# Later weight sums, another unit order and shifted forms in a one-core transformer layer

## The chip, the cores and the metric

The kernel runs on one core of one Trainium2 chip. The metric is the device time of one execution in microseconds; the number given for a kernel is the median of its runs. A profiled execution is a separate run, recorded instruction by instruction; its own time stands beside the span that the profile covers.

## The reference

One layer for 272 tokens (16 learned meta tokens ahead of 256 real ones) of 2048 features: a SwiGLU half-step, a mixer with two kinds of attention, and a second SwiGLU half-step. The meta tokens are dropped at the end. All is float32.

```
h = concatenate([meta, x])
h = h + 0.5 * swiglu(rmsnorm(h, ffn1_norm), w_gate1, w_up1, w_down1)     # D_FF = 5632
h = h + hybrid_mixer(rmsnorm(h, mix_norm), w_in, ..., w_out)             # fox + stick-breaking heads
h = h + 0.5 * swiglu(rmsnorm(h, ffn2_norm), w_gate2, w_up2, w_down2)
swiglu(x) = (silu(x @ w_gate) * (x @ w_up)) @ w_down
```

## The kernel before, in words

**Units.** All weight matrices are read once, in units of 128 x 1024 float32 values (512 KB). `load` (line 1118) brings a unit from memory into a `raw` tile by a DMA on SP's queue. `split_unit` (line 1131) makes two halves of it in a reduced float format: `wh`, a rounded copy by ScalarE (lines 189 and 1136), and `wl = raw - wh` by VectorE (lines 190 and 1142). `products` (line 1174) multiplies: for every float32 product TensorE runs three matmuls, high by high, high by low and low by high. `wh` and `wl` have three buffers each, so a copy into one waits for the unit three places earlier. The loop at the end calls `ahead(u)` and `products(u)` for every unit `u`; `ahead` (line 1232) loads 6 units ahead (9 in the second half-step) and splits 2 units ahead. `raw` has 5 buffers, and 3 more in the second half-step.

**Order.** The list `units` gives the order in which the program is traced. The framework's scheduler then orders each engine's instructions by that priority and by its own estimate of when operands are ready, so an instruction can come before others that were traced earlier. Each engine's queue runs in order, SP's with its DMAs too. `tc.issue_after(i)` keeps what follows behind instruction `i` on `i`'s queue. The first units are traced under a manual schedule for ScalarE and VectorE.

**First half-step.** 264 units of 24 matmuls with 272 columns. `first_norm` and `first_start` (lines 360 and 373) bring x in, transpose it and make its halves while the first eight weight units arrive; `first_factors` makes the norm's factors.

**Weight sums.** In the second half-step the gate and up products of eight column groups (`SEVENS`) go by seven half-size products in place of eight (Strassen's scheme in Winograd's form). It needs three sums of weight quarters per group and row block. `weight_sums` (line 1055) makes them during the first half-step: for each of 32 sets three loads into `pre` tiles (line 1079), three VectorE subtractions (lines 1067, 1069 and 1071) and three stores to scratch memory (line 1061). The generator yields 6 times per set; `ahead` advances it by `SUMS_PACE` = 0.8 steps per unit, from the first call (unit 7) to the mixer. The `pre` tiles lie in a memory phase that the attention's tiles take over (line 156 writes the first of them).

**Second half-step.** The activations come in seven `forms` (`normal_forms`, line 868): quarters `a11`, `a12`, `a22` and combinations `s1` to `s4`, each as a high and a low half; `a21` is for the plain groups. The first four are `f` tiles of the phase "second half-step" (`F_BUFS` = 8), the others lie in the general `v` slots. A group is 28 product units (`Group.ORDER`): four of p1, four of p5, four times p6, p2, p4, four of p3 and four of p7, each with 6 matmuls of 512 columns (line 1012). p4 loads nothing: its weights are p6's raw minus p2's (line 1141, VectorE, in place), so p6 and p2 are its providers. The plain work is done in units of 12 matmuls (line 1205): the gate and up blocks of groups 0, 1 and 7, and the down product, which is cut into parts (`PART`, in groups of four 128-row tiles) of four column blocks each. Every down block ends in two evictions by VectorE (`down2`, line 942). The list takes seven product units, then three plain units, and so on; 24 plain units remain for the end. Finished gate-up tiles are transposed by TensorE and split (`turn`, line 431).

```
ORDER = ([("p1", u) for u in range(4)] + [("p5", u) for u in range(4)]
         + [(p, u) for u in range(4) for p in ("p6", "p2", "p4")]
         + [("p3", u) for u in range(4)] + [("p7", u) for u in range(4)])
FORM = {"p1": "a11", "p2": "a12", "p3": "s4", "p4": "a22", "p5": "s1", "p6": "s2", "p7": "s3"}
```

Of the kernel before, what the change touches and what calls it, by code (L numbers as in the profile page):

```python
# [8 lines left out]
F32 = mybir.dt.float32  # L9
# [7 lines left out]
P = 128  # L17
# [15 lines left out]
SPLIT_BUFS = 3  # L33
LOAD_AHEAD = 6
SECOND_AHEAD = 9
SUMS_PACE = 0.8
PRE_BUFS = 9
F_BUFS = 8
SPLIT_AHEAD = 2
# [12 lines left out]
def hybrid_layer(ctx: ExitStack, tc: tile.TileContext, x, meta_tokens, ffn1_norm, ffn1_w_gate, ffn1_w_up,  # L52
                 ffn1_w_down, mix_norm, w_in, b_forget, fox_q_norm, fox_k_norm, w_branch_fox, w_branch_sb,
                 w_out, ffn2_norm, ffn2_w_gate, ffn2_w_up, ffn2_w_down, out):
    nc = tc.nc
# [6 lines left out]
    def phase(title):  # L62

        if phases:
            phases.pop().release()
        if title:
            phases.append(tc.alloc_tile_pool(name=title, reuse_waits="tile"))
# [10 lines left out]
    def name(tag):  # L78
        uid[0] += 1
        return f"{tag}_{uid[0]}"  # L80

    def slot(shape, dt):
        return vp.tile(shape, dt, tag="v", name=name("v"))
# [4 lines left out]
    def ptile(shape, dt, tag, bufs=1):  # L88
        return phases[-1].tile(shape, dt, tag=tag, name=name(tag), bufs=bufs)
# [21 lines left out]
    def drain(*which):  # L111
        while any(lanes[k] for k in which):
            tick()
# [19 lines left out]
    def tables():  # L133
        return tc.keep_in_program_order(act.preload_act_table_set(LN_EXP)).ins
# [296 lines left out]
    def turn(u, dest, t0):  # L431

        yield 6
        for j0 in range(0, 4, 2):
            p = aux()
            for j in range(2):
                for i in range(2):
                    c = (j0 + j) * P
                    pe.transpose(p[:, (2 * j + i) * P:(2 * j + i + 1) * P], u[:, i, c:c + P], ident[:])  # L439
            h = slot([P, 2, 2, NR], F32R)  # L440
            split(h[:, :, 0, :], h[:, :, 1, :], p[:].rearrange("p (j t) -> p j t", j=2))
            dest[(t0 + j0) // 2] = h
            yield 2
# [360 lines left out]
    def open_gates(kind):  # L804
        drain("prep", "attend")

        def sigmoids():
            for c in range(4):
                g = gates[kind, c]
                with tc.issue_after(exps[-1].ins):  # L810
                    act.activation(g[:], g[:], AF.Sigmoid)
                yield 10
            if kind == "f":
                tables()
        lanes["misc"].append(sigmoids())
        if kind == "s":
            phase("second half-step")

    def branch_rhs(kind):
        return lambda kt: o_slots[kind, kt // 2][:, kt % 2, :, :]  # L820
# [13 lines left out]
    for c in range(4):  # L834
        blocks.append(Block(w_branch_fox[0], 0, 8, c * 512, 512, branch_rhs("f"), NR, branch_evac("f", c), True,
                            before=(lambda: open_gates("f")) if c == 0 else None))
# [14 lines left out]


    SEVENS = (2, 3, 4, 5, 6, 8, 9, 10)
    PART = (1, 2, 2, 2, 2, 2)
    acc = {}
    forms = {}

# [91 lines left out]
    def plain_group(g):  # L949

        u = {}
        factor = lambda i: norms["ffn2"].rtok[:, i:i + 1] if g == 0 else 1.0

        def ev_gate(i, ps):
            if i == 0:
                u["t"] = slot([P, 2, 512], F32)
            assert norms["ffn2"].done
            act.activation(u["t"][:, i, :], ps[:], AF.Silu, scale=factor(i))

        def ev_up(i, ps):  # L960
            s = u["t"][:, i, :]
            if g == 0:
                dve.scalar_tensor_tensor(s, ps[:], factor(i), s, op0=ALU.mult, op1=ALU.mult)
                free["g0"] = i == 1
            else:
                dve.tensor_tensor(s, ps[:], s, op=ALU.mult)
            if i == 1:
                lanes["turn"].append(turn(u["t"], hs2, 4 * g))

        def rhs(kt):  # L970
            if g == 0:
                return norms["ffn2"].rhs(kt)
            return [[forms[f"a{i + 1}{kt // 8 + 1}"][m][:, kt % 8, :] for i in range(2)] for m in range(2)]

        return [Block(w[0], 0, KT, g * 512, 512, rhs, NR, ev, True)
                for w, ev in ((ffn2_w_gate, ev_gate), (ffn2_w_up, ev_up))]

    def down_blocks(t0, count, last):
        return [Block(ffn2_w_down[0], t0 * P, count, c * 512, 512,
                      lambda kt: hs2[(t0 + kt) // 2][:, kt % 2, :, :], NR,  # L980
                      lambda i, ps, c=c: down2(last, c, i, ps), True) for c in range(4)]
# [66 lines left out]
    def weights_of(w, half, u, g):  # L1048

        r = (8 * half + 2 * u) * P  # L1050
        return w[r:r + 2 * P, g * 512:(g + 1) * 512].rearrange("(k p) c -> p k c", p=P)
# [3 lines left out]
    def weight_sums():  # L1055

        last = None

        def store(group, u, ts, i):
            d = dp.tile([P, 1024], F32, tag=f"sum{group.g}_{i}_{u}", name=f"sum{group.g}_{i}_{u}")  # L1060
            nc.sync.dma_start(d[:], ts[i][:].rearrange("p k c -> p (k c)"))
            group.sums[i, u] = d

        def add(ts, i):
            t1, t3, t2 = ts
            if i == 0:
                dve.tensor_tensor(t1[:], t3[:], t1[:], op=ALU.subtract)  # L1067
            elif i == 1:
                dve.tensor_tensor(t3[:], t2[:], t3[:], op=ALU.subtract)
            else:  # L1070
                dve.tensor_tensor(t2[:], t2[:], t1[:], op=ALU.subtract)

        work = [(group, u) for group in groups.values() for u in range(4)]
        for group, u in work + [(None, 0)]:
            ts = []
            for i, (w, half) in enumerate(((ffn2_w_gate, 0), (ffn2_w_up, 0), (ffn2_w_up, 1))):
                if group:
                    t = ptile([P, 2, 512], F32, "pre", PRE_BUFS)
                    nc.sync.dma_start(t[:], weights_of(w[0], half, u, group.g))
                    ts.append(t)  # L1080
                if last and i:
                    add(last[2], i)
                yield
            for i in range(3):
                if last:
                    store(*last, i)
                if group and i == 2:
                    add(ts, 0)
                yield
            last = (group, u, ts) if group else None  # L1090

    ahead_sums = weight_sums()


    def units_of(bs):
        return [(b, k0, 1024 // b.cols) for b in bs for k0 in range(0, b.kts, 1024 // b.cols)]

    units = units_of(blocks)
    second = len(units)
    mixer = next(u for u, (b, _, _) in enumerate(units) if b.w is wi)  # L1100
    units += units_of(plain_group(0))
    seven = [(groups[g], p, u) for g in sorted(groups) for p, u in Group.ORDER]
    starts = [4 * sum(PART[:i]) for i in range(len(PART))]
    down = [down_blocks(t0, 4 * n, t0 + 4 * n == FT) for t0, n in zip(starts, PART)]
    eight = [down[0], plain_group(1), *down[1:3], plain_group(7), *down[3:]]
    eight = [u for bs in eight for u in units_of(bs)]
    while seven or eight:
        units += seven[:7]
        units += eight[:3]
        del seven[:7], eight[:3]  # L1110
    raws, halves, banks = {}, {}, {}

    def raw_tile(shape):
        if loaded >= second and loaded % 8 >= RAW_BUFS:
            return ptile(shape, F32, "raw", 8 - RAW_BUFS)
        return wp.tile(shape, F32, tag="raw", name=name("raw"), bufs=RAW_BUFS)

    def load(u):
        b, k0, n = units[u]
        if isinstance(b, Group):  # L1120
            if k0 != "p4":
                t = raw_tile([P, 2, 512])
                nc.sync.dma_start(t[:], b.source(k0, n))
                raws[u] = t
            return
        t = raw_tile([P, n, b.cols])
        rows = slice(b.row0 + k0 * P, b.row0 + (k0 + n) * P)
        nc.sync.dma_start(t[:], b.w[rows, b.col0:b.col0 + b.cols].rearrange("(k p) c -> p k c", p=P))
        raws[u] = t

    def split_unit(u):
# [99 lines left out]

    def ahead(u):
        nonlocal loaded, done, sums_due
        if u < mixer - 2:
            sums_due += SUMS_PACE
            while sums_due >= 1:
                sums_due -= 1
                next(ahead_sums, None)
        while loaded < min(len(units), u + (LOAD_AHEAD if u < second else SECOND_AHEAD)):
            load(loaded)  # L1240
            loaded += 1
        while done < min(len(units), u + 1 + SPLIT_AHEAD):
            split_unit(done)
            done += 1
# [13 lines left out]
    for c in range(1, KT // 2):  # L1258
        with tc.issue_after(meta.ins):
            load_x(c)  # L1260
            load(c)
# [52 lines left out]
```

## Time and profile before

| | |
|---|---|
| runs before | median 2251.82 us of 3 (2251.27 to 2252.03) |
| profiled execution | 2251.66 us, its span 2249.9 us |
| TensorE matmuls | 2220.2 us busy, 13740 |
| VectorE | 1569.0 us busy |
| ScalarE | 1155.5 us busy |
| DMA | 537.30 MB, mean 239 GB/s |

In the profile PE is TensorE's matmuls, PEld its weight loads, DVE VectorE, ACT ScalarE, POOL GpSimd and SP the engine that issues most DMAs. A timeline row gives the start, the duration, the engine, the line, what is written and what is read, and in brackets the idle time before it and what ended that. A row of waits gives who waited for whom, the total, how many times and the longest. A row of windows gives the stretch, its length, the busy time and the number of instructions of each engine, the granted TensorE clock as a share of full speed, the share of DMA time and the rate. A matmul's recorded duration overlaps that of the next, so the distance of starts is the time that it takes.

### The profile page before, as it was taken

The page shows a single profiled execution, that of the slowest core. Times are in us where ns is not written, and L with a number is a line of the kernel's source. Part 1 is how long each engine was busy: PE and PEld are TensorE (multiplying, and loading weights), DVE is VectorE, ACT ScalarE, POOL GpSimd, SP SyncE. Part 2 cuts the span into 40 slices and gives each one's busy share as a digit, 9 for nine tenths or more (in the row PEclk, how much of TensorE's full clock was granted, in tenths as well). Part 3 has the DMA queues.
Part 4 walks back from the last instruction along what each step waited for, and adds up shares of the span by engine and source line. Part 5 has one row for each costly group of instructions (what it writes and reads, how often), then busy time and mean ns, then how long its engine had stood idle before and what let it go on. Part 6 is the DMA issues. An engine that isn't in the chain of part 4 may idle for free.

```text
span 2249.9 us, 34780 instructions
## 1 busy us (share of the span) xinstructions
PE 2220.2 (99%) x13740; PEld 2002.8 (89%) x13740; DVE 1569.0 (70%) x1904; ACT 1155.5 (51%) x1447; POOL 42.8 (2%) x112
## 2 busy tenths in 40 slices
PE   7999999999999999999999999999999999999999
PEld 7999999999999999998899988887777777777787
DVE  6767766667755565988556565668878878778774
ACT  4444443334443454666445565458666666666653
POOL 0000000000000000110000000000000000000000
PEclk8999999999999999999999999999999999999999
DMA  8999999999985556555655456555777777877774
GB/s 306 327 326 323 341 328 332 335 332 329 333 285 176 178 172 190 165 158 168 190 181 158 150 149 209 181 185 165 239 260 262 238 240 261 264 238 235 262 248 135
DMA packets 256388, 537.30 MB, mean 239 GB/s; under 512 B 16777, under 2 KB 21729, under 8 KB 256225
## 3 DMA queue, kind: packets, MB, share of 16 engines
q1 hardware_dynamic: 254144, 531.56, 72.4%
q8 instruction: 107, 1.75, 0.3%
q10 hardware_dynamic: 1472, 2.37, 0.3%
q0 software_dynamic: 608, 1.16, 0.2%
q14 instruction: 57, 0.46, 0.1%
HBM read 482.58 MB, written 52.44 MB: 238 GB/s over the span
## 4 chain that ended last, share of the span: by engine, by line
PE 93%; DVE 3%; ACT 1%; issue 1%; DMA 1%; ACTq 0%; DVEq 0%
PE acc L1205 80%; PE acc L1012 10%; DVE wl L1142 2%; ACT wh L1136 1%; PE aux L726 1%; DVE raw L1141 1%; PE aux L599 1%; PE aux L439 1%; DMA pre<-in_ffn_w_up_dram 0%; DMA v<-in_x_dram 0%; DVE wl L190 0%; PE aux L587 0%; PE aux L697 0%; DVE f L190 0%; PE aux L864 0%
## 5 line engine op out<-in xcount | busy, mean ns | idle before, releaser
L1205 PE MATMUL acc<-v,wh 128*128 128x272 f32 (+1 forms) x5776 | 1175.1, 299 | 1.2 <-ACT wh L189 1.2
L190 DVE TENSOR_TENSOR wl<-raw,wh 128x1024 fp32r<-128x1024 f32 (+1 forms) x625 | 760.9, 1222 | 419.2 <-ACT wh L189 416.8
L189 ACT ACTIVATE wh<-raw 128x1024 fp32r<-128x1024 f32 (+1 forms) x625 | 660.2, 1058 | 763.4 <-PE acc L1205 672.2
L1205 PEld LDWEIGHTS acc<-v,wh 128*128 128x128 f32 x5776 | 925.8, 189 | 24.2 <-ACT wh L189 1.4
L1205 PE MATMUL acc<-v,wl 128*128 128x272 f32 (+1 forms) x3128 | 898.4, 288 | 9.5 <-DVE wl L190 9.5
L1205 PEld LDWEIGHTS acc<-v,wl 128*128 128x128 f32 x3128 | 589.0, 189 | 9.8 <-DVE wl L190 9.7
L1205 PE MATMUL acc<-wh,v 128*128 128x512 f32 x1728 | 557.6, 394 | 2.7 <-ACT wh L189 2.7
L1205 PEld LDWEIGHTS acc<-wh,v 128*128 128x128 f32 x1728 | 323.4, 188 | 72.0 <-ACT wh L189 4.6
L1142 DVE TENSOR_TENSOR wl<-raw,wh 128x1024 fp32r<-128x1024 f32 x224 | 273.2, 1224 | 104.2 <-ACT wh L1136 97.9
L1205 PE MATMUL acc<-wl,v 128*128 128x512 f32 x864 | 338.5, 392 | 0.9 <-DVE wl L190 0.9
L1136 ACT ACTIVATE wh<-raw 128x1024 fp32r<-128x1024 f32 x224 | 236.8, 1061 | 185.4 <-PE acc L1205 121.9
L1205 PEld LDWEIGHTS acc<-wl,v 128*128 128x128 f32 x864 | 162.3, 188 | 36.1 <-DVE wl L190 3.7
L1012 PE MATMUL acc<-wh,f 128*128 128x512 f32 x512 | 168.1, 396 | 0.0
L1012 PE MATMUL acc<-wh,v 128*128 128x512 f32 x384 | 127.2, 396 | 7.3 <-ACT wh L1136 7.3
L1012 PEld LDWEIGHTS acc<-wh,f 128*128 128x128 f32 x512 | 96.2, 188 | 22.6
L1012 PE MATMUL acc<-wl,f 128*128 128x512 f32 x256 | 101.8, 398 | 0.0
L1012 PEld LDWEIGHTS acc<-wh,v 128*128 128x128 f32 x384 | 72.1, 188 | 28.5 <-ACT wh L1136 14.2
L1012 PE MATMUL acc<-wl,v 128*128 128x512 f32 x192 | 76.8, 400 | 0.0
L1067 DVE TENSOR_TENSOR pre<-pre,pre 128x1024 f32<-128x1024 f32 x32 | 39.2, 1224 | 45.9 <-DMA pre<-in_ffn_w_up_dram 45.8
L1012 PEld LDWEIGHTS acc<-wl,f 128*128 128x128 f32 x256 | 48.1, 188 | 12.2 <-DVE wl L1142 1.5
L1012 PEld LDWEIGHTS acc<-wl,v 128*128 128x128 f32 x192 | 36.0, 187 | 12.2 <-DVE wl L1142 4.5
L1205 PE MATMUL acc<-wh,f 128*128 128x512 f32 x128 | 45.9, 399 | 0.9 <-ACT wh L189 0.9
(259 smaller groups left out, 1223.9 us busy)
## 6 DMA issues: line engine op xcount, KB each, us to landing
raw<-in_ffn_w_down_dram SPq DMA_DIRECT2D x176, 512.0 KB, 4.8
raw<-in_ffn_w_gate_dram SPq DMA_DIRECT2D x175, 512.0 KB, 5.2
raw<-in_w_in_dram SPq DMA_DIRECT2D x162, 512.0 KB, 3.7
raw<-in_ffn_w_up_dram SPq DMA_DIRECT2D x144, 512.0 KB, 5.3
sum<-pre SPq DMA_DIRECT2D x96, 512.0 KB, 6.3
raw<-sum SPq DMA_DIRECT2D x96, 512.0 KB, 4.8
pre<-in_ffn_w_up_dram SPq DMA_DIRECT2D x64, 512.0 KB, 6.7
pre<-in_ffn_w_gate_dram SPq DMA_DIRECT2D x32, 512.0 KB, 7.0
```

The source lines that it names most:

```text
L189: act.activation(hi, src, AF.Copy)
L190: dve.tensor_tensor(lo, src, hi.bitcast(F32), op=ALU.subtract)
L439: pe.transpose(p[:, (2 * j + i) * P:(2 * j + i + 1) * P], u[:, i, c:c + P], ident[:])
L599: pe.matmul(po[:, :NR], a[:, ks], b[:, i * NR:(i + 1) * NR], start=n == 0, stop=n == 6)
L726: pe.matmul(o, a, b, start=start, stop=stop, skip_group_check=True)
L1012: pe.matmul(ps[:], a[:, kt, :], b[:, i, :], start=fresh and kt == 0 and m == 0, stop=kt == 7 and m == 2, skip_group_check=True)
L1067: dve.tensor_tensor(t1[:], t3[:], t1[:], op=ALU.subtract)
L1136: act.activation(wh[:], raw[:], AF.Copy)
L1141: dve.tensor_tensor(t[:], t[:], raw[:], op=ALU.subtract)
L1142: dve.tensor_tensor(wl[:], raw[:], wh[:].bitcast(F32), op=ALU.subtract)
L1205: pe.matmul(o, a, c, start=first and m == 0, stop=last and m == len(terms) - 1, skip_group_check=wide)
```

## The change

Five edits. The sums start with unit 20 at 0.84 steps per unit, and each of their loads stays behind the newest weight load on SP's queue. A `[128, 48]` float32 tile is set to zero on POOL when the phase "second half-step" opens; it takes 192 bytes per partition ahead of that phase's other tiles. The down product has five parts (3, 2, 2, 2, 2) in place of six. Plain group 1 now comes ahead of the first down part. And one plain unit stands after every p2, and after every second unit of p1, p5, p3 and p7, which gives 12 plain units per 28 product units as before, and again 24 at the end.

```
-SUMS_PACE = 0.8
+SUMS_PACE = 0.84
+SUMS_FROM = 20
...
             phase("second half-step")
+            nc.gpsimd.memset(ptile([P, 48], F32, "shift")[:], 0.0)
...
-    PART = (1, 2, 2, 2, 2, 2)
+    PART = (3, 2, 2, 2, 2)
...
-                    nc.sync.dma_start(t[:], weights_of(w[0], half, u, group.g))
+                    with tc.issue_after(newest[0]):
+                        nc.sync.dma_start(t[:], weights_of(w[0], half, u, group.g))
...
-    eight = [down[0], plain_group(1), *down[1:3], plain_group(7), *down[3:]]
+    eight = [plain_group(1), *down[:2], plain_group(7), *down[2:]]
     eight = [u for bs in eight for u in units_of(bs)]
-    while seven or eight:
-        units += seven[:7]
-        units += eight[:3]
-        del seven[:7], eight[:3]
-    raws, halves, banks = {}, {}, {}
+    for g, p, u in seven:
+        units.append((g, p, u))
+        if p == "p2" or p in ("p1", "p5", "p3", "p7") and u % 2:
+            units.append(eight.pop(0))
+    units += eight
+    raws, halves, banks, newest = {}, {}, {}, []
...
-        nc.sync.dma_start(t[:], b.w[rows, b.col0:b.col0 + b.cols].rearrange("(k p) c -> p k c", p=P))
+        q = nc.sync.dma_start(t[:], b.w[rows, b.col0:b.col0 + b.cols].rearrange("(k p) c -> p k c", p=P))
+        newest[:] = [q.ins]
...
-        if u < mixer - 2:
+        if SUMS_FROM <= u < mixer - 2:
```

## The prediction

> **What bounds the kernel now.** I read the page first, then the waits of the first 56 us, the timelines of that stretch, and then the windows and timelines of the eight weight-sum groups of the second half-step.
>
> ```profile
> span 2249.9 us, 34780 instructions
> PE 2220.2 (99%) x13740; PEld 2002.8 (89%) x13740; DVE 1569.0 (70%) x1904; ACT 1155.5 (51%) x1447; POOL 42.8 (2%) x112
> ```
>
> TensorE sets the end. Matmuls overlap in the records, so 99% hides short waits and slow spacing; I look for time at which the starts of matmuls lie further apart than their steady distance. The first such place is the start. The waits of 12 to 56 us, then VectorE's and TensorE's timelines there:
>
> ```profile
> PEld acc L1205 <- DVE wl L190: 9.7, 1, 9.7
> DVE pre L1067 <- DMA pre<-in_ffn_w_up_dram: 8.8, 1, 8.8
> ```
>
> ```profile
> 20.62 1.23 DVE L1067 TENSOR_TENSOR pre<-pre,pre 128x1024 f32<-128x1024 f32 x1 [8.83 <-DMA pre<-in_ffn_w_up_dram]
> 21.76 1.22 DVE L190 TENSOR_TENSOR wl<-raw,wh 128x1024 fp32r<-128x1024 f32 x1
> ...
> 34.92 0.75 DVE L358 COPY v<-aux 128x256 f32<-128x256 f32 x2
> 35.59 0.86 DVE L347 SCALAR_TENSOR_TENSOR v<-aux,gcol,v 128x256 fp32r<-128x256 f32 x2
> 36.37 0.18 DVE L354 TENSOR_TENSOR v<-v,v 128x32 fp32r<-128x32 f32 x1
> 36.63 1.23 DVE L190 TENSOR_TENSOR wl<-raw,wh 128x1024 fp32r<-128x1024 f32 x1
> ```
>
> ```profile
> 12.27 1.26 PE L1205 MATMUL acc<-v,wh 128*128 128x272 f32 x8
> 23.04 0.60 PE L1205 MATMUL acc<-v,wl 128*128 128x272 f32 x1 [9.50 <-DVE wl L190]
> ...
> 31.19 0.50 PE L1205 MATMUL acc<-v,wh 128*128 128x272 f32 x2
> ...
> 34.63 0.87 PE L1205 MATMUL acc<-v,wh 128*128 128x272 f32 x5
> ```
>
> The reader is to see a queue blocked at its head: the first weight sum (L1067) stands on VectorE in front of the low half of the second weight unit (L190), waits 8.83 us for its own load, and TensorE waits 9.50 us for that low half. The second place is the groups: the windows of all eight groups, and the chain of one fourth product.
>
> ```profile
> 1575.74:2180.00 604.26, 593.43 (x2583) 472.94 (x2582) 486.51 (x462) 372.91 (x394) 0.00 (x0) 1.00 0.76 251
> ```
>
> ```profile
> 1601.24 1.22 DVE L1141 TENSOR_TENSOR raw<-raw,raw 128x1024 f32<-128x1024 f32 x1
> 1603.67 1.23 DVE L1142 TENSOR_TENSOR wl<-raw,wh 128x1024 fp32r<-128x1024 f32 x1 [1.21 <-ACT wh L1136]
> ```
>
> ```profile
> 1602.58 1.06 ACT L1136 ACTIVATE wh<-raw 128x1024 fp32r<-128x1024 f32 x1 [2.51 <-DVE raw L1141]
> ```
>
> ```profile
> 1602.90 0.39 PE L1012 MATMUL acc<-wh,f 128*128 128x512 f32 x1
> 1603.69 0.49 PE L1012 MATMUL acc<-wh,v 128*128 128x512 f32 x1 [0.40 <-ACT wh L1136]
> ```
>
> VectorE subtracts (L1141), ScalarE copies (L1136), and only then can p4's product begin, 0.79 us after the matmul before it.
>
> **Part one: the sums leave the start.** What the start loses is worked out from TensorE in 12.27 to 55.41 us, from the second unit's first matmul to the tenth's: first L1205's matmuls alone, with a steady stretch, then all of TensorE's, then all engines in the bad pieces.
>
> ```profile
> 12.27:55.41 43.14, 30.06 (x193) 0.84 0.93 317
> 100.00:400.00 300.00, 300.00 (x2392) 1.00 0.96 330
> ```
>
> ```profile
> 12.27:55.41 43.14, 32.18 (x224) 0.84 0.93 317
> ```
>
> ```profile
> 23.04:27.50 4.46, 4.46 (x20) 4.46 (x21) 3.57 (x9) 0.00 (x1) 0.00 (x0) 0.50 0.83 274
> 44.80:48.40 3.60, 2.14 (x12) 1.38 (x11) 3.49 (x13) 3.33 (x6) 0.00 (x0) 1.00 1.00 269
> 48.50:51.80 3.30, 3.30 (x16) 3.30 (x16) 3.30 (x5) 0.00 (x0) 0.00 (x0) 0.50 0.99 375
> ```
>
> A steady matmul takes 300/2392 = 125.4 ns, so 193 take 24.2 us; the 31 others take 32.18 - 30.06 = 2.1 us; 43.14 - 24.2 - 2.1 = 16.8 us are lost. Of them 9.5 us are the wait above, and (4.46 + 3.30)/2 = 3.9 us go because the granted clock is 0.50 in two windows that follow a wait; the rest, 3.4 us, is mostly the stretch from 44.80, where TensorE is busy for 2.14 of 3.60 us. With the first 20 units free of sums, all three loads, stores and adds of a set move behind them. The loads are also tied behind the newest weight load on SP's queue, so they cannot drift forward again. On VectorE a starting unit then costs 0.75 + 0.86 + 0.18 + 1.23 = 3.02 us, against 34.63 - 31.19 = 3.44 us on TensorE, which is the next bound. The second unit's low half still waits for ScalarE, some 0.3 us, and the norm's factors behind the seventh unit keep about 2.5 us (estimate). Gain 14; ends 9.5 (only the one wait goes) and 16.8 (all).
>
> The Trainium skill (TensorE: Matmul & The Clock Gate, Part 1) has the clock halved after an idle window of about 3.4 us. Here the second halving follows a stretch with TensorE busy for 2.14 of 3.60 us, so the trace is harsher than the page; by the page a leftover stall of 1 us costs only itself.
>
> Later the sums end later. The generator has 198 steps; at 0.84 a unit from unit 20 the last falls at about unit 256 of the mixer's 264, some 8 units of 24 x 125.4 ns = 3.01 us, or 24 us, ahead of it.
>
> ```profile
> POOL pw L156 <- DMA sum<-pre: 613.5, 1, 613.5
> ...
> DVE pre L1067 <- DMA pre<-in_ffn_w_up_dram: 45.8, 25, 8.8
> ```
>
> ```profile
> sum<-pre SPq DMA_DIRECT2D x96, 512.0 KB, 6.3
> ```
>
> The attention tiles (pw first) take the sums' memory and wait for the stores; these land in 6.3 us, inside the 24. The traffic is 1.84 x 0.524 MB per 3.01 us = 320 GB/s, under the 330 that the steady row carries with TensorE fully busy. I take 0 for this; the other end is the slow rival below.
>
> **Part two: the order of the groups, and five down parts.** From the page's groups and from the lines, and two stretches of the same line with nine matmuls each, first with an f form, then with a form in a v slot; last a turn:
>
> ```profile
> L1142 DVE TENSOR_TENSOR wl<-raw,wh 128x1024 fp32r<-128x1024 f32 x224 | 273.2, 1224 | 104.2 <-ACT wh L1136 97.9
> ...
> L942 DVE SCALAR_TENSOR_TENSOR v<-acc,v 128x512 f32<-128x512 f32 (+1 forms) x50 | 31.0, 661 | 5.0 <-PE acc L1205 5.0
> ```
>
> ```profile
> 1580.17 0.39 PE L1012 MATMUL acc<-wl,f 128*128 128x512 f32 x1
> ...
> 1582.27 0.40 PE L1012 MATMUL acc<-wl,f 128*128 128x512 f32 x1
> ```
>
> ```profile
> 1633.10 0.39 PE L1012 MATMUL acc<-wl,v 128*128 128x512 f32 x1
> ...
> 1635.14 0.39 PE L1012 MATMUL acc<-wl,v 128*128 128x512 f32 x1
> ```
>
> ```profile
> 1582.74 0.60 PE L439 MATMUL aux<-ident,v 128*128 128x128 f32 x4
> 1583.09 0.48 PE L1012 MATMUL acc<-wh,f 128*128 128x512 f32 x1
> ```
>
> Nine matmuls take 2.10 us with f (233.3 ns each) and 2.04 with v (226.7). Eight groups hold 8 x (28 x 6 + 12 x 12) = 2496 products, 960 of them with f (four of seven forms, 768; group 7's, 192). 960 x 233.3 + 1536 x 226.7 = 572.2 us; the other 87 of the 2583 are turns, 22 fours of 0.35 us, 7.7. Of 604.26 us, 24.4 are therefore waits.
>
> Why: in p6, p2, p4 VectorE has four passes, 4 x 1.224 = 4.90 us, and TensorE 18 matmuls, 4.08. In a run of seven such units nothing pays the difference back in time, because splits run only two units ahead with three buffers. With a plain unit after p2, TensorE has 6.80 us and VectorE five passes, 6.12. The three buffers let a copy start when the unit three places earlier is done: p4 and p6 then have a product unit and a plain one, 4.08 us, and p2 and the plain unit have two product units, 2.72 us, for 1.06 + 1.22 = 2.28. That is enough but tight: a down eviction of 0.66 us, or the subtraction in the wrong place, still shows. I let 9.4 of 24.4 stay: gain 15; ends 8 and 22. The raws have landed long before, and p6's is held by one plain unit (2.72 us) longer; three loads per 6.80 us are 231 GB/s, less than the 251 of the row above.
>
> Five parts instead of six drop 4 blocks of 2 evictions, 8 x 0.66 = 5.3 us of VectorE. VectorE is busy 486.51 of 604.26 us, so this is priced at nothing by itself; the wait it eases is in the 15.
>
> **Part three: the 192 bytes.** By the program's addresses the weight halves and the v slots begin 192 bytes past a multiple of 256, the f tiles on one; the change puts these 192 past it too. If that is what separates 233.3 from 226.7, it gives 960 x 6.6 ns = 6.3 us; if placement is no cause, 0. The two stretches differ in nothing else that I see, so I take 5. The POOL memset that makes the room has no reader, and POOL's queue behind it is empty in the groups (0.00 us in their row).
>
> The Trainium skill (TensorE: Matmul & The Clock Gate, Part 2) speaks against this gain: two independent read ports, so loading the next weights takes no bandwidth from the running matmul. By it the sum would be 5 us less.
>
> **Sum.** 14 + 15 + 5 = 34 us off the profiled execution's 2251.66 us, which lies 0.16 under the median of the three runs: 2217.7, with the median 2217.8; I say 2218.
>
> **Rivals.** *Placement is no cause*: 2223; for it, only the page's two ports; against it, the two stretches. *The start meets its next wait*: only 9.5 of 14 come, 2222; for it, 3.02 of 3.44 us of VectorE per unit. *The groups stay bound by VectorE*: 6.12 of 6.80 plus evictions; only 4 of 15, 2229. *The order does not become what is written*, the scheduler draws sums and units together again: about 2250; against it, the tie to the weight load.
>
> *Slower: sums block VectorE throughout the first half-step.* The loads now sit behind weight loads which themselves wait for buffers, so an add may stand at VectorE's head for longer. Beyond the first, 24 waits of L1067 took 37.0 us, 1.5 each, and cost TensorE nothing: a low half has two units, 6.0 us, for 2.3 us of work, 3.7 us of cover. Were the waits of the 32 sets 4.8 us on average, TensorE would lose 32 x 1.1 = 35 us and the gain is gone; at 5.5 us it loses 58, and the time is 2276.
>
> **Chances.** Forecast 0.58, placement 0.12, start 0.08, groups 0.14, order 0.03, slower 0.05. The range 2209 to 2235 takes in the first four with their bounds (the high end: groups at 8, placement at 0, start at 9.5 is 2234); the low end adds three quarters of what the upper bounds (16.8, 22, 6.3) give beyond 34. A measurement of this kernel can tell about 0.2%, 4.5 us, from no change. Faster by more: 0.92; within it: 0.03; slower: 0.05.
>
> **What would show it.** In the profile after: no L1067 before some 70 us and no half-clock window behind it; the tenth unit's first matmul near 41 us; the last sum store near 780 us; a group in about 73 us in place of 75.5; nine f matmuls in 2.04 us. Wrong would be: TensorE waiting for a low half in the first 100 us again, waits of L1067 over 4 us, groups above 75 us, or f matmuls still at 233 ns.

## The result and the profile after

| | before | after |
|---|---|---|
| median | 2251.93 us (4 runs) | 2212.40 us (4 runs) |
| profiled execution | 2251.66 us, span 2249.9 | 2213.04 us, span 2211.3 |

The ratio is 0.9824, with a 95% interval of 0.9807 to 0.9841: 39.5 us less. The forecast was 2218, with 34 us less. Between the two profiles lie 38.6 us, and three marks split them. The tenth unit's first matmul comes at 41.51 us in place of 55.41, the first group of the second half-step at 1561.85 in place of 1575.74: 13.9 us from the start, and nothing between the two marks. The other 24.7 us come after 1561.85.

The lines of the changed kernel have moved: the sums stand at L1069, L1071 and L1073, the subtraction for p4 at L1146, group products at L1014, other products at L1210, `wl` at L191 and L1147, `wh` at L190 and L1141. First the head of the page:

```profile
span 2211.3 us, 34800 instructions
PE 2203.9 (100%) x13740; PEld 2003.5 (91%) x13740; DVE 1567.7 (71%) x1896; ACT 1158.1 (52%) x1447; POOL 42.4 (2%) x113
```

The start, on VectorE and on TensorE:

```profile
13.53 1.23 DVE L191 TENSOR_TENSOR wl<-raw,wh 128x1024 fp32r<-128x1024 f32 x1 [0.48 <-ACT wh L190]
...
80.38 1.22 DVE L1069 TENSOR_TENSOR pre<-pre,pre 128x1024 f32<-128x1024 f32 x1
```

```profile
13.80 1.24 PE L1210 MATMUL acc<-v,wh 128*128 128x272 f32 x8
14.88 0.32 PE L1210 MATMUL acc<-v,wl 128*128 128x272 f32 x1
```

The second unit's low half is made at 13.53 us, and its first matmul follows the high-half ones without idle time, where 9.50 us stood before. The first sum is at 80.38 us. The windows come next. The first row, with the granted clock at 0.50 ahead of the second unit, is new; the other two answer to rows shown before:

```profile
8.80:12.20 3.40, 3.34 (x16) 3.32 (x16) 2.18 (x7) 0.75 (x3) 0.77 (x4) 0.50 1.06 387
...
44.80:48.40 3.60, 3.60 (x31) 3.60 (x30) 1.22 (x1) 1.65 (x2) 0.00 (x0) 1.00 0.61 161
...
1561.85:2141.30 579.45, 579.45 (x2578) 475.07 (x2577) 482.55 (x451) 374.68 (x392) 0.00 (x0) 1.00 0.80 261
```

The eight groups end after 579.45 us in place of 604.26, with TensorE's records closed up throughout. The sums' end, as the waits and SP's timeline show it:

```profile
POOL pw L157 <- DMA sum<-pre: 751.0, 1, 751.0
...
DVE pre L1069 <- DMA pre<-in_ffn_w_up_dram: 22.6, 21, 2.8
```

```profile
759.77 0.34 SPq L1063 DMA_DIRECT2D sum<-pre  x1
```

The last store is issued at 759.77 us, 51 us ahead of the mixer's first matmul (810.31). The forecast was near 780, some 24 us ahead of it; why the stores run earlier was not followed up. The waits of the first sum fell from 45.8 to 22.6 us; the slow rival, sums that block VectorE, did not come. Last the subtractions on VectorE, and nine matmuls with an f form and nine with a v slot on TensorE:

```profile
1589.85 1.23 DVE L1146 TENSOR_TENSOR raw<-raw,raw 128x1024 f32<-128x1024 f32 x1
1596.65 1.22 DVE L1146 TENSOR_TENSOR raw<-raw,raw 128x1024 f32<-128x1024 f32 x1
1603.45 1.23 DVE L1146 TENSOR_TENSOR raw<-raw,raw 128x1024 f32<-128x1024 f32 x1
```

```profile
1562.08 0.39 PE L1014 MATMUL acc<-wl,f 128*128 128x512 f32 x1
...
1564.12 0.39 PE L1014 MATMUL acc<-wl,f 128*128 128x512 f32 x1
...
1610.64 0.39 PE L1014 MATMUL acc<-wl,v 128*128 128x512 f32 x1
...
1612.68 0.39 PE L1014 MATMUL acc<-wl,v 128*128 128x512 f32 x1
```

The subtractions come every 6.80 us: 30 matmuls of 226.7 ns, TensorE's own time for p6, p2, a plain unit and p4. Nine f matmuls take 2.04 us, as many as nine v matmuls.

### The profile page after: what moved, and what is told of

The parts are those of the page before. It is cut to its first block, busy times and chain, and to the rows that moved or that the text cites. A ratio compares the mean times of both kernels' runs of the same rounds, so it can differ in the third digit from the quotient of the medians.

```text
span 2211.3 us, 34800 instructions
## 1 busy us (share of the span) xinstructions
PE 2203.9 (100%) x13740; PEld 2003.5 (91%) x13740; DVE 1567.7 (71%) x1896; ACT 1158.1 (52%) x1447; POOL 42.4 (2%) x113
## 4 chain that ended last, share of the span: by engine, by line
PE 99%; DVE 1%; DMA 0%; issue 0%; ACT 0%; SPq 0%; DVEq 0%
PE acc L1210 81%; PE acc L1014 14%; PE aux L727 1%; PE aux L600 1%; PE aux L440 1%; PE aux L588 0%; PE aux L698 0%; DMA v<-in_meta_tokens_dram 0%; DVE wl L191 0%; PE acc L1176 0%; DVE f L191 0%; PE aux L866 0%; PE aux L340 0%; ACT wh L190 0%; PE aux L677 0%
## 5 line engine op out<-in xcount | busy, mean ns | idle before, releaser
L1210 PE MATMUL acc<-v,wh 128*128 128x272 f32 (+1 forms) x5776 | 1172.8, 298 | 0.0
L191 DVE TENSOR_TENSOR wl<-raw,wh 128x1024 fp32r<-128x1024 f32 (+1 forms) x625 | 763.6, 1223 | 481.5 <-ACT wh L190 476.2
L190 ACT ACTIVATE wh<-raw 128x1024 fp32r<-128x1024 f32 (+1 forms) x625 | 661.5, 1059 | 827.1 <-PE acc L1210 742.2
L1210 PEld LDWEIGHTS acc<-v,wh 128*128 128x128 f32 x5776 | 923.5, 189 | 22.7
L1210 PE MATMUL acc<-v,wl 128*128 128x272 f32 (+1 forms) x3128 | 897.0, 287 | 0.0
L1210 PEld LDWEIGHTS acc<-v,wl 128*128 128x128 f32 x3128 | 587.4, 188 | 0.2
L1210 PE MATMUL acc<-wh,v 128*128 128x512 f32 x1728 | 562.2, 392 | 0.0
L1210 PEld LDWEIGHTS acc<-wh,v 128*128 128x128 f32 x1728 | 324.5, 188 | 67.1
L1210 PE MATMUL acc<-wl,v 128*128 128x512 f32 x864 | 339.7, 393 | 1.0 <-DVE wl L191 1.0
L1147 DVE TENSOR_TENSOR wl<-raw,wh 128x1024 fp32r<-128x1024 f32 x224 | 272.0, 1223 | 28.2 <-ACT wh L1141 18.3
L1141 ACT ACTIVATE wh<-raw 128x1024 fp32r<-128x1024 f32 x224 | 236.7, 1061 | 94.1 <-PE acc L1014 43.4
L1210 PEld LDWEIGHTS acc<-wl,v 128*128 128x128 f32 x864 | 162.3, 188 | 38.8 <-DVE wl L191 6.6
L1014 PE MATMUL acc<-wh,f 128*128 128x512 f32 x512 | 168.7, 390 | 0.0
L1014 PE MATMUL acc<-wh,v 128*128 128x512 f32 x384 | 127.5, 389 | 0.0
L1014 PEld LDWEIGHTS acc<-wh,f 128*128 128x128 f32 x512 | 96.1, 188 | 20.0
L1014 PE MATMUL acc<-wl,f 128*128 128x512 f32 x256 | 99.6, 389 | 0.0
L1014 PEld LDWEIGHTS acc<-wh,v 128*128 128x128 f32 x384 | 72.1, 188 | 14.9
L1014 PE MATMUL acc<-wl,v 128*128 128x512 f32 x192 | 74.8, 390 | 0.0
L1014 PEld LDWEIGHTS acc<-wl,f 128*128 128x128 f32 x256 | 48.1, 188 | 9.9
L1069 DVE TENSOR_TENSOR pre<-pre,pre 128x1024 f32<-128x1024 f32 x32 | 39.2, 1224 | 22.8 <-DMA pre<-in_ffn_w_up_dram 22.6
L1071 DVE TENSOR_TENSOR pre<-pre,pre 128x1024 f32<-128x1024 f32 x32 | 39.1, 1223 | 10.0 <-DMA pre<-in_ffn_w_up_dram 9.8
L1210 PE MATMUL acc<-wh,f 128*128 128x512 f32 x128 | 44.9, 391 | 0.0
```

The lines of the kernel that those rows point to most:

```text
L190: act.activation(hi, src, AF.Copy)
L191: dve.tensor_tensor(lo, src, hi.bitcast(F32), op=ALU.subtract)
L1014: pe.matmul(ps[:], a[:, kt, :], b[:, i, :], start=fresh and kt == 0 and m == 0, stop=kt == 7 and m == 2, skip_group_check=True)
L1141: act.activation(wh[:], raw[:], AF.Copy)
L1147: dve.tensor_tensor(wl[:], raw[:], wh[:].bitcast(F32), op=ALU.subtract)
L1210: pe.matmul(o, a, c, start=first and m == 0, stop=last and m == len(terms) - 1, skip_group_check=wide)
```

## The experiments

My theory: three causes that hardly touch each other. The start lost its time because the scheduler drew a sum in front of a weight's low half; the groups because VectorE's work came in bunches; the f matmuls because of where their tile lies against the moving one. Rivals: the plain unit helps by its distance between p2 and p4; the later start in the text helps by itself; only the stationary tile's own place counts.

**The sums alone**, on the kernel before: start, pace and tie.

```
+SUMS_PACE = 0.84
+SUMS_FROM = 20
...
+                    with tc.issue_after(newest[0]):
...
+        if SUMS_FROM <= u < mixer - 2:
```

> The kernel before with the sums' edits alone: start at unit 20, pace 0.84, loads tied behind the newest weight load. If the three parts add up, the whole 13.9 us by which the changed kernel reaches its tenth unit earlier is here, and the groups take 75.5 us each as before: 2238.0 us. Rival, sums that end 130 us later cost something in the first half-step: the mixer's first unit is reached less than 13.9 us earlier, and the time is above 2241.

Measured 2237.11 us against 2250.26 (ratio 0.9939, 0.9924 to 0.9954). The mixer's first unit comes at 809.53 us in place of 824.20, and the stretch from the tenth unit to it takes 768.80 us, against 768.79 before. The later end of the sums costs nothing.

**The tie alone**: sums from unit 7 at pace 0.8.

```
+                    with tc.issue_after(newest[0]):
+                        nc.sync.dma_start(t[:], weights_of(w[0], half, u, group.g))
...
```

> The kernel before with the tie alone: sums from the first call (unit 7) at pace 0.8, their loads behind the newest weight load. If the tie does the work, the 9.5 us wait is gone, as the first sum cannot come before the eighth unit's load, and only some of the later 3 us of waits (44.8 to 48.4 us) stays: 2238 to 2242 us. If the 20 units matter as such, the first sums still hold up VectorE while the norm's factors are made: 2244 us or more.

Measured 2237.80 us against 2251.28 (0.9942, 0.9925 to 0.9958): as much as all three edits of the sums. VectorE's timeline shows why the 20 units don't matter:

```profile
43.77 1.23 DVE L1067 TENSOR_TENSOR pre<-pre,pre 128x1024 f32<-128x1024 f32 x1 [2.53 <-DMA pre<-in_ffn_w_up_dram]
```

The first sum moves from 20.62 to 43.77 us by the tie alone. It still waits 2.53 us there, which TensorE doesn't feel.

**No tie**: the changed kernel with loads that may go anywhere, though they still begin with unit 20.

```
-                    with tc.issue_after(newest[0]):
-                        nc.sync.dma_start(t[:], weights_of(w[0], half, u, group.g))
+                    nc.sync.dma_start(t[:], weights_of(w[0], half, u, group.g))
```

> The changed kernel without the tie of the sums' loads to the newest weight load; they still begin with unit 20 in the program's text. If the scheduler is free to pull them forward into SP's idle time, the first sum is again in front of the second weight unit's low half, TensorE waits some 9.5 us there, and the whole 13.9 us of the start are lost: 2226 us. If the later start in the text is enough, 2212.4 us.

Measured 2226.53 us against 2251.28 (0.9891, 0.9876 to 0.9906), 14.1 us above the changed kernel. VectorE and TensorE at the start:

```profile
20.39 1.23 DVE L1069 TENSOR_TENSOR pre<-pre,pre 128x1024 f32<-128x1024 f32 x1 [8.67 <-DMA pre<-in_ffn_w_up_dram]
21.54 1.22 DVE L191 TENSOR_TENSOR wl<-raw,wh 128x1024 fp32r<-128x1024 f32 x1
```

```profile
22.81 0.59 PE L1209 MATMUL acc<-v,wl 128*128 128x272 f32 x1 [9.34 <-DVE wl L191]
```

The sum is back in front, at the same place as before the change. So the tie moves the sums; the later start in the text does nothing without it, and with it adds nothing that these runs can tell (2237.11 against 2237.80 us).

**The order alone**, with the five parts:

```
-    PART = (1, 2, 2, 2, 2, 2)
+    PART = (3, 2, 2, 2, 2)
...
+    eight = [plain_group(1), *down[:2], plain_group(7), *down[2:]]
...
+    for g, p, u in seven:
+        units.append((g, p, u))
+        if p == "p2" or p in ("p1", "p5", "p3", "p7") and u % 2:
+            units.append(eight.pop(0))
...
```

> The kernel before with the unit order and the five down parts alone. If the waits in the groups come from VectorE's four passes against three product units, and the plain unit pays them back, the groups lose about 18.5 us together and the start stays as it was: 2233.4 us. Rival, most of the gain of the groups came with the shifted forms: over 2240 us.

Measured 2232.49 us against 2250.26 (0.9918, 0.9903 to 0.9933). **The 192 bytes alone**:

```
             phase("second half-step")
+            nc.gpsimd.memset(ptile([P, 48], F32, "shift")[:], 0.0)
```

> The kernel before with the 192 bytes alone. Nine matmuls with an f form should start within 2.04 us in place of 2.10. If the parts were independent, 960 x 6.5 ns = 6.2 us come off: 2245.7 us. If VectorE sets the pace in p6, p2, p4, the f matmuls there (8 units of 6 in each of eight groups, 384 of 960) only wait longer, and 3.7 us come off: 2248.2 us. If placement is no cause, f matmuls stay at 233 ns and the time at 2251.9 us.

Measured 2246.43 us against 2250.26 (0.9981, 0.9971 to 0.9990). Both of the non-zero expectations lie in that interval; the windows of the first seven groups decide. In order: before, shift alone, order alone, changed.

```profile
1575.74:2105.48 529.74, 520.24 (x2266) 414.57 (x2265) 426.06 (x405) 326.93 (x346) 0.00 (x0) 1.00 0.76 251
```

```profile
1574.04:2100.06 526.02, 515.73 (x2265) 414.31 (x2264) 425.60 (x405) 326.89 (x346) 0.00 (x0) 1.00 0.77 252
```

```profile
1575.70:2088.48 512.78, 512.78 (x2258) 416.09 (x2256) 421.39 (x393) 328.28 (x344) 0.00 (x0) 1.00 0.80 258
```

```profile
1561.85:2068.94 507.09, 507.09 (x2257) 415.71 (x2256) 421.19 (x393) 328.36 (x344) 0.00 (x0) 1.00 0.80 261
```

By itself the shift takes 3.7 us off seven groups; on top of the order it takes 512.78 - 507.09 = 5.7. Seven groups hold 7 x 96 + 192 = 864 f matmuls, and 864 x 6.6 ns is 5.7. Without p6 and p2 they are 528, or 3.5 us. This fits the second expectation: where VectorE sets the pace, a shorter matmul only waits longer. The kernel with the shift alone has its short matmuls and its waits on the subtraction side by side; the last row is TensorE's wait for p4's copy:

```profile
1574.26 0.39 PE L1013 MATMUL acc<-wl,f 128*128 128x512 f32 x1
...
1576.30 0.39 PE L1013 MATMUL acc<-wl,f 128*128 128x512 f32 x1
```

```profile
ACT wh L1137 <- DVE raw L1142: 31.2, 16, 2.8
...
PE acc L1013 <- ACT wh L1137: 8.2, 16, 0.7
```

The same two rows of the kernel before:

```profile
ACT wh L1136 <- DVE raw L1141: 30.6, 16, 2.8
...
PE acc L1012 <- ACT wh L1136: 7.3, 16, 0.7
```

Nine in 2.04 us, and the waits are still there: ScalarE's 31.2 us behind VectorE in place of 30.6, TensorE's 8.2 us in place of 7.3. The rows go the way of the explanation, but show only 0.9 of the 2.2 us (336 matmuls of p6 and p2 at 6.6 ns) that it asks for. The three parts by themselves give 13.2 + 17.8 + 3.8 = 34.8 us against their own runs of before; together 39.5. Of the 4.7 us between, this overlap explains some 2 (5.7 - 3.7); 1.7 lie in the runs of before themselves, whose median is 2251.93 us beside the changed kernel and 2250.26 beside the parts; the rest is of the size of the intervals.

**The plain unit behind p4**, with p4 right behind its providers:

```
-        if p == "p2" or p in ("p1", "p5", "p3", "p7") and u % 2:
+        if p == "p4" or p in ("p1", "p5", "p3", "p7") and u % 2:
```

> The changed kernel with the plain unit behind p4 in place of behind p2, so that p4 follows its providers at once, with the same mixture of units. If what counts is VectorE's work per stretch (five passes, 6.12 us, against 6.80 us of TensorE), nothing changes: 2212.4 us within 3. If what counts is the distance between p2 and p4, each of 32 p4 waits 0.4 to 0.8 us as before: 2225 to 2238 us.

Measured 2212.60 us against 2250.26 (0.9829, 0.9815 to 0.9844), and the seven groups:

```profile
1561.17:2068.16 506.99, 506.99 (x2257) 415.52 (x2256) 420.04 (x393) 328.55 (x344) 0.00 (x0) 1.00 0.80 261
```

506.99 against 507.09 us. The distance between providers and user is not what helps; what the two orders share is the plain unit in each round of p6, p2 and p4.

**Six parts** in the new order (plain group 1 still first):

```
-    PART = (3, 2, 2, 2, 2)
+    PART = (1, 2, 2, 2, 2, 2)
...
-    eight = [plain_group(1), *down[:2], plain_group(7), *down[2:]]
+    eight = [plain_group(1), *down[:3], plain_group(7), *down[3:]]
```

> The changed kernel with six down parts (1, 2, 2, 2, 2, 2), all else in its order. If the eight evictions that five parts save on VectorE lie beside other work, as priced, nothing moves: 2212.4 us within 1. If they fall into the tight stretch p6, p2, p4, each of eight blocks costs up to 0.7 us: 2214 to 2218 us.

Measured 2212.76 us against 2251.10 (0.9830, 0.9812 to 0.9847). The eight evictions more are seen on VectorE (x401 against x393) and not in the time. No run tries the earlier place of plain group 1 by itself. The seven groups with six parts:

```profile
1561.45:2068.51 507.06, 507.06 (x2258) 415.62 (x2256) 424.97 (x401) 328.13 (x344) 0.00 (x0) 1.00 0.79 260
```

**Where the tiles lie.** First 128 bytes in place of 192:

```
-            nc.gpsimd.memset(ptile([P, 48], F32, "shift")[:], 0.0)
+            nc.gpsimd.memset(ptile([P, 32], F32, "shift")[:], 0.0)
```

> The changed kernel with 128 bytes in place of 192. If places modulo 256 bytes decide, f matmuls start 234 to 235 ns apart, as matmuls with v tiles at that place do in the kernel before (235 ns), and the time is about 2218 us. If 192 bytes only broke up some other overlap, they stay at 227 ns.

```profile
1560.71 0.39 PE L1014 MATMUL acc<-wl,f 128*128 128x512 f32 x1
...
1562.77 0.39 PE L1014 MATMUL acc<-wl,f 128*128 128x512 f32 x1
```

One run, 2213.25 us; nine matmuls in 2.06 us, 228.9 ns. The place counts, but the expected 234 to 235 ns and 2218 us were wrong. Then the weight halves were moved, by 64, 128 and 192 bytes, with all later pools and without the v slots:

```
     phase("sums")
+    nc.gpsimd.memset(wp.tile([P, 16], F32, tag="shift", name="wshift", bufs=1)[:], 0.0)    # 32, 48
```

> The changed kernel with 64 bytes ahead of the weight halves: these and all later pools move by 64, the v slots don't. Weight halves and f forms then both begin on a multiple of 256, the v slots 192 past one. If the spacing depends on where the stationary tile lies against the moving one, f stays at 227 ns, the forms in v slots go from 227 to about 231 to 235 ns, and with 2656 such matmuls the time rises by 10 to 20 us, the first half-step aside. If it depends on the stationary tile's own place, f goes back to 233 ns and v stays at 227: about 2218 us.

> The changed kernel with 128 bytes ahead of the weight halves (all later pools move with them, the v slots don't). With 64 bytes the first half-step from unit 20 to the mixer took 732.62 us in place of 735.25, and f stayed at 227 ns. If places relative to each other decide, f stays at 227 ns here too, the v forms leave 227 ns, and the first half-step takes something other than 735.25 us. If not, f goes to another distance.

> The same with 192 bytes: f at 227 ns by relative place, the v forms at another distance than 227, the first half-step from unit 20 to the mixer between 730 and 738 us.

With 64 bytes 2212.80 us against 2251.28 (0.9833, 0.9818 to 0.9848), where 10 to 20 us more than the changed kernel's were expected; with 128 and 192 one run each, 2223.44 and 2234.53 us. An f and a v stretch of the kernel with 64, a v stretch of that with 128 and one of that with 192:

```profile
1571.52 0.39 PE L1015 MATMUL acc<-wl,f 128*128 128x512 f32 x1
...
1573.56 0.39 PE L1015 MATMUL acc<-wl,f 128*128 128x512 f32 x1
...
1608.36 0.39 PE L1015 MATMUL acc<-wl,v 128*128 128x512 f32 x1
...
1610.42 0.39 PE L1015 MATMUL acc<-wl,v 128*128 128x512 f32 x1
```

```profile
1771.73 0.39 PE L1015 MATMUL acc<-wl,v 128*128 128x512 f32 x1
...
1773.82 0.39 PE L1015 MATMUL acc<-wl,v 128*128 128x512 f32 x1
```

```profile
1769.41 0.39 PE L1015 MATMUL acc<-wl,v 128*128 128x512 f32 x1
...
1771.51 0.40 PE L1015 MATMUL acc<-wl,v 128*128 128x512 f32 x1
```

With f and the weight halves both on a multiple of 256, nine f matmuls take 2.04 us, as with both 192 past one; in the kernel before, f lay on that same multiple, the halves 192 past it, and they took 2.10. The stationary tile's own place is thus not the cause: its place against the moving tile, modulo 256 bytes, is. Weight halves 0, 64, 128 and 192 bytes further on than the stationary tile go with 2.04, 2.06 (f with 128 bytes, v with 64), 2.09 (v with 128) and 2.10 us (f before, v with 192). Places between these steps of 64 bytes were not measured. TensorE alone, from unit 20 to the mixer, for the changed kernel and for 64, 128 and 192 bytes:

```profile
75.06:810.31 735.25, 735.25 (x5858) 1.00 0.91 312
```

```profile
74.33:806.95 732.62, 731.71 (x5858) 1.00 0.91 313
```

```profile
73.93:809.18 735.25, 735.25 (x5858) 1.00 0.90 312
```

```profile
75.31:817.07 741.76, 741.76 (x5858) 1.00 0.89 309
```

The first half-step depends on it too, and is shortest at 64: 2.6 us less than in the changed kernel, or 0.45 ns a matmul. So equal places are not the best for every matmul: in the first half-step the weight halves are the stationary tiles, the v tiles the moving ones, and there are 272 columns; which of these differences matters was not tried. The expectations that 128 would differ from 735.25, and that 192 would lie between 730 and 738, were wrong. With 64 the second half-step gives the gain back, as its v slots now lie wrongly.

**A version that keeps both**: 64 bytes ahead of the weight halves, and the 4096-byte stationary tiles 64 bytes into their v slots.

```
+    def placed(shape, dt):
+        t = slot([P, 1088], dt)[:, 16:1040]
+        return t.rearrange("p (a b c) -> p a b c", a=2, b=2) if len(shape) == 4 else t.rearrange("p (k c) -> p k c", k=8)
...
-            h = slot([P, 2, 2, NR], F32R)
+            h = placed([P, 2, 2, NR], F32R)
...
```

> The kernel of weights_64 with the 4096-byte high and low tiles of the v slots (later forms, transposed halves, attention outputs, the second norm's parts) placed 64 bytes into their slots of 4352 bytes. If only the place relative to the weight halves counts, these 2528 matmuls return from 229.5 to 227.7 ns, the first half-step keeps the 2.6 us that weights_64 gained there, and the profile ends 4 to 7 us before that of weights_64, some 4 us before the changed kernel's: 2207 to 2209 us. If the stationary tile's own place counts, they stay at 229.5 ns or get slower: 2213 us or more.

Measured 2208.57 us against 2251.16 (0.9811, 0.9798 to 0.9825, 5 runs; 2207.75 to 2208.97). The changed kernel's runs lay at 2211.33 to 2213.04; against their own runs of before the two gain 42.6 and 39.5 us. The v stretch is back at 2.04 us, and the first half-step is shorter still:

```profile
1606.56 0.39 PE L1019 MATMUL acc<-wl,v 128*128 128x512 f32 x1
...
1608.60 0.39 PE L1019 MATMUL acc<-wl,v 128*128 128x512 f32 x1
```

```profile
75.06:805.98 730.92, 730.92 (x5859) 1.00 0.89 314
```

Of the 735.25 us, 4.3 are gone. Of these 2.6 were expected. Another 0.9 is idle time of TensorE that the kernel with 64 bytes had there (731.71 busy of 732.62) and this one has not; where the last 0.8 (731.71 to 730.92) comes from stays open, since the first half-step's own high and low tiles lie as in the kernel with 64 bytes.

## Why the prediction was right

**The start, 14 us forecast, 13.9 measured.** The wait, what ended it and its price were as written. That the sum came out to 0.1 us was partly luck. From the second unit's first matmul to the tenth's the changed kernel takes 27.71 us in place of 43.14, and TensorE has no idle time there: 15.4 of the 16.8 us are gone, and 1.4 stay. Some 2.8 us were forecast to stay, as waits for the low half and the norm's factors, which do not show. What brings the gain back to 13.9 is that the second unit starts 1.53 us later (13.80 against 12.27), behind the window at half clock from 8.80 us; with the plain unit behind p4, whose run has no such window, it starts at 12.90.

```profile
13.80:41.51 27.71, 27.71 (x223) 27.29 (x222) 25.10 (x58) 23.14 (x68) 0.00 (x0) 1.00 0.68 217
```

The second half-clock window, too, was read as a consequence of the stretch before it. The kernel with the shift alone has the start of before, and a stretch like that, but no half clock after it:

```profile
43.10:46.70 3.60, 2.26 (x17) 1.82 (x15) 3.50 (x12) 3.29 (x8) 0.00 (x0) 1.00 0.93 300
...
48.50:51.80 3.30, 3.19 (x25) 2.97 (x25) 3.30 (x6) 0.75 (x1) 0.00 (x0) 1.00 1.03 395
```

It makes 25 matmuls from 48.50 to 51.80 us where the profile of before made 16, and its second half-step starts 1.7 us earlier (1574.04 against 1575.74). So the wait alone does not bring that term of 1.65 us; it comes in one run and not in another. One reason was put too widely: I gave the gain to the 20 units and called the tie a safeguard. The runs show the tie to be all of it (2237.80 us alone, against 2237.11 with all three edits). The price of nothing for the later end of the sums held: 768.80 against 768.79 us.

**The order, 15 us forecast, 18.4 measured**, from the first group to the end of the span (674.2 us before, 655.8 with the order alone). The mechanism was right: four passes of VectorE against three units of TensorE in a round, five against five with a plain unit. What was mis-sized is what stays. I let 9.4 of 24.4 us stay, since 2.28 us of work in 2.72 looked too tight for an eviction beside it; 6.0 stayed. The subtractions every 6.80 us show that nothing is lost in such a round, and the six parts, with eight evictions more, that these find room. Closed records do not mean that nothing is left: in the changed kernel's eight groups weight loads of plain units still wait for VectorE's low halves:

```profile
PEld acc L1210 <- DVE wl L191: 5.3, 16, 0.4
```

In some 50 places of these groups two matmuls of 512 columns start 0.27 to 0.34 us apart in place of 0.227, 4.9 us together (3.5 with the order alone). They may be most of the 6.0; that they come from this wait is not shown. The five parts are worth nothing, as priced. The forecast's count of 960 f products is right, its label is not: the 192 outside the product units belong to groups 1 and 7, 96 each.

**The place, 5 us forecast, 6.3 measured** on top of the order (655.8 to 649.5 us), which is the upper end; by itself, on the kernel before, the shift gave 3.8. The two stretches were right against the page. The Trainium skill (TensorE: Matmul & The Clock Gate, Part 2) has two independent read ports, so that loading the next weights takes nothing from the running matmul. Here the place of one operand's tile against the other's changes the distance of the matmuls from 226.7 to 233.3 ns, so in these runs the spacing goes by both places together. Which part of the chip makes it so was not shown.

**The rivals.** The start's next wait, groups that stay bound, an order undone by the scheduler and sums that block VectorE did not come. What the order rival feared is real for the sums in the kernel without the tie: 14.1 us.

## What to carry to other kernels

Where a scheduler orders an engine's queue by estimated readiness, a later place in the text does not keep side work out of the start; an explicit tie to the work that must come first does. When two engines share a pipeline with two units of run-ahead, spread the units that are light for the tighter engine singly among the heavy ones: the sum over a hundred units may fit, and a run of seven still waits. Once TensorE is closed up, look at the distance of its starts by operand tile: the same matmul of 512 columns took 1 to 3% longer with its stationary tile at another place against the moving one.

## What the runs showed of the hardware that I had not expected

The place of the tiles, above: moving the weight halves by 0 to 192 bytes changed the whole kernel from 2212 to 2234 us (one run each for 128 and 192), with the same matmuls.

The granted clock halves at the start at different times in runs of the same start. In the changed kernel it is 0.50 from 8.80 to 12.20 us (shown above, 16 matmuls); with the plain unit behind p4, whose start is the same, it is not:

```profile
8.80:12.20 3.40, 3.40 (x24) 3.40 (x24) 2.69 (x7) 1.26 (x4) 0.77 (x4) 1.00 1.06 388
```

24 matmuls in place of 16 in the same 3.40 us, so about a microsecond of a single run's time is chance. The Trainium skill (TensorE: Matmul & The Clock Gate, Part 1) has the clock's window run freely, so that its phase against the kernel's start varies; these two rows agree with that. The half-clock window at 48.50 us, which came before the change and not with the shift alone, is a second case, of 1.7 us.
